# A rank scatter limited by its DMA engines: skipped partitions in five groups, a reset in place of a drain, and ranks from two counts per column

## The chip, the cores and the metric

The kernel runs on one core of a Trainium2 chip. The metric is device time in microseconds (us) per execution. The median before the change is 775.2 us (four runs, 775.0 to 775.73; the first three of them gave 775.31). Smaller is better. Changes are compared with the kernel before on the same chip and in the same rounds. Everything read from a trace comes from one profiled execution of that kernel, and its times count from the start of the span. A run that takes over 1.5% more than the fastest of its kernel is classed slow; ratios use the other runs alone, the fast ones.

## The reference

```python
B, N, D = 8, 2048, 2560                 # x: [B, N, D] fp32, scores: [B, N] fp32

def reference(x, scores):
    order = np.argsort(scores, axis=1)
    ranks = np.argsort(order, axis=1)
    out = np.zeros_like(x)
    b_idx = np.arange(B)[:, None]
    out[b_idx, ranks, :] = x
    return out
```

Each row of 2560 floats (10,240 bytes) goes to the place that its score has in the sorted order of its batch. A row's rank is the number of smaller scores in its batch plus the number of equal scores at smaller positions.

## The kernel before

A batch of 2048 rows is eight groups of 256 rows; a group fills 128 partitions with two rows each. Two kinds of traffic move the rows:

- "Bulk" groups are loaded into one of eight buffers and scattered from there. Pool issues both on one queue, in order, and each scatter waits for the ranks of its batch.
- Group 0 of batches 0 to 5, and the rows of skipped partitions ("holes"), are copied from HBM to HBM one row at a time by the sync engine (SP) and the scalar engine (ACT), 800 rows each. I call them direct rows.

The Vector engine counts the ranks, one column of 128 rows at a time, with every score of the batch spread over all partitions in `s_all`:

```python
THIN = {**{(b, 4): 48 for b in range(1, B)}, (7, 5): 44}   # (batch, group): first skipped partition
HALVED = range(32)                                         # groups loaded in two halves
STEPS = [(0, 1), (1, 2), (2, 4), (4, 8)]                   # groups ranked together, batch 0 only
# ... (cut)
count(0, lo, C, nc.vector.tensor_scalar,                   # later scores: smaller ones
      scalar1=score, scalar2=None, op0=OP.is_lt, op1=OP.add)
if lo:
    count(1, 0, lo, nc.vector.tensor_scalar,               # earlier scores: smaller or equal
          scalar1=score, scalar2=None, op0=OP.is_le, op1=OP.add)
count(2, lo, lo + m, nc.vector.scalar_tensor_tensor,       # equal scores inside the group, masked
      scalar=score, in1=mask[...], op0=OP.is_equal, op1=OP.mult)
# ... (cut)
steps = STEPS if b == 0 else [(0, len(GROUPS))]            # later batches: one step of 16 columns
```

Pool's order of work is one program:

```python
for k in range(1, NBUF):                                   # NBUF = 8 buffers
    load_ahead(k)
for k, (b, g) in enumerate(BULK):
    if k >= LAG and k + NBUF - LAG < len(BULK):            # LAG = 4
        scatters_done(pl, k - LAG)
        load_ahead(k + NBUF - LAG)
    pl.wait(*loaded[k])
    pl.after(dve, t_bulk[b, g])                            # the ranks of (b, g)
    for j in range(GROUPS[g][1]):
        scatter(k, j)
nc.gpsimd.drain()
for k in range(max(0, len(BULK) - NBUF), len(BULK)):
    scatters_done(sp, k)
```

Pool holds everything behind one wait for ranks, loads of later groups too. While it waits, the DMA engines live on what is queued already.

## Time and profile before

| kernel before | |
|---|---|
| time, median | 775.2 us |
| profiled span | 772.8 us |
| rate after the first slice | about 418 GB/s |
| Vector engine busy | 400.7 us, done at about 437 us |
| median landing of the last scatter | 766.6 us, the latest of its sixteen engines 770.6 us |

The page's row of slices divides the span into 40 equal parts; one digit is the busy share in tenths. The prediction shows those rows, the queues, and Pool's wait for batch 1. Beyond them I need the page's line of busy time (engine, us, share of the span, number of instructions) and its costliest group (mean ns of one before the second bar):

```profile
PE 36.2 (5%) x172; PEld 30.4 (4%) x172; DVE 400.7 (52%) x828; ACT 0.0 (0%) x1; POOL 164.6 (21%) x213
L239 DVE TENSOR_SCALAR_CACHE_REDUCE trash<-s_all,s_col 128x1792 bf16<-128x1792 f32 (+7 forms) x240 | 315.2, 1348 | 4.6
```

The counts are most of the Vector engine's work, and no engine is busy for the whole span.

### The profile page before, as it was taken

Reading aid. Unit: us, or ns where it says so; the run is one execution under the profiler, and the core shown is the slowest. Engines: PE = TensorE matmul, PEld = TensorE weight load, DVE = VectorE, ACT = ScalarE, POOL = GpSimd, SP = SyncE. Lnnn points to the kernel's source line nnn. Section 1 sums busy time; section 2 is a strip of 40 time slices with the busy share of each in tenths; the row PEclk is TensorE's granted clock in tenths of the full one; section 3 lists DMA queues with packets and bytes.
Section 4 is the critical chain, followed back from the end, with each engine's and each line's share of the span. In section 5 each row is a group of like instructions: output and inputs, shape, how many; then the busy total and the mean of one; then the engine's idle time right before and its main releaser. Section 6 shows DMA issues by size and latency. Waiting matters only on the chain.

```text
span 772.8 us, 8228 instructions
## 1 busy us (share of the span) xinstructions
PE 36.2 (5%) x172; PEld 30.4 (4%) x172; DVE 400.7 (52%) x828; ACT 0.0 (0%) x1; POOL 164.6 (21%) x213
## 2 busy tenths in 40 slices
PE   4000020020020020030000000000000000000000
PEld 3000010010010010030000000000000000000000
DVE  5999979979979979979999500000000000000000
ACT  0000000000000000000000000000000000000000
POOL 4114223222213131312112121212121212112100
PEclk8555555555555555565555555555555555555555
DMA  8999999999999999999999999999999999999996
GB/s 358 418 418 420 418 418 418 418 417 418 418 420 417 420 417 417 419 417 419 416 421 421 422 416 426 416 427 417 422 417 424 417 426 415 424 418 424 419 414 283
DMA packets 80898, 320.15 MB, mean 414 GB/s; under 512 B 28968, under 2 KB 54568, under 8 KB 54568
## 3 DMA queue, kind: packets, MB, share of 16 engines
q0 software_dynamic: 29376, 300.82, 91.7%
q1 hardware_dynamic: 25904, 10.93, 5.2%
q10 hardware_dynamic: 25600, 8.24, 4.3%
q14 instruction: 17, 0.14, 0.0%
q8 instruction: 1, 0.02, 0.0%
HBM read 168.49 MB, written 168.43 MB: 436 GB/s over the span
## 4 chain that ended last, share of the span: by engine, by line
DMA 63%; DVE 13%; another core or an unknown queue 9%; POOL 6%; issue 4%; PE 1%; POOLq 0%; SPq 0%
DMA out_dram<-x,rank_i 57%; DVE trash L239 12%; DMA x<-in_x_dram 6%; POOL out_dram L424 4%; POOL x L126 2%; PE ps_all L196 0%; DVE s_all L341 0%; DMA s_in<-in_scores_dram 0%; PE ps_col L175 0%; POOLq L448 0%; DVE rank_i L277 0%; DVE rank L271 0%; DVE rank L265 0%; PE ps_row L300 0%
## 5 line engine op out<-in xcount | busy, mean ns | idle before, releaser
L239 DVE TENSOR_SCALAR_CACHE_REDUCE trash<-s_all,s_col 128x1792 bf16<-128x1792 f32 (+7 forms) x240 | 315.2, 1348 | 4.6
L424 POOL DMA_INDIRECT out_dram<-x,rank_i x116 | 113.4, 977 | 139.6 <-issue 35.0
L126 POOL DMA_DIRECT2D x<-in_x_dram x88 | 49.4, 565 | 436.9 <-DMA out_dram<-x,rank_i 418.5
L239 DVE SCALAR_TENSOR_TENSOR trash<-s_all,s_col,mask 128x256 bf16<-128x256 f32 x128 | 61.6, 482 | 0.0
L196 PE MATMUL ps_all<-ident,s_col 128*128 128x128 f32 x128 | 28.1, 411 | 3.2 <-DVE s_all L341 2.8
L300 PE MATMUL ps_row<-ident,rank 128*1 128x128 f32 x28 | 8.3, 398 | 393.6 <-DVE rank_i L286 386.4
L196 PEld LDWEIGHTS ps_all<-ident,s_col 128*128 128x128 f32 x128 | 26.5, 222 | 4.2 <-DVE s_all L341 3.2
L341 DVE COPY s_all<-ps_all 128x512 f32<-128x512 f32 x32 | 20.2, 685 | 1.5 <-PE ps_all L196 1.1
L239 DVE DVE_READ_ACCUMULATOR trash<-s_all,s_col 128x1 f32 x240 | 19.9, 83 | 0.0
L300 PEld LDWEIGHTS ps_row<-ident,rank 128*1 128x1 f32 x28 | 2.0, 97 | 397.9 <-DVE rank_i L286 389.5
L311 DVE TENSOR_SCALAR thin_i<-ps_row 1x8 int32<-1x8 f32 x8 | 1.2, 154 | 19.0 <-PE ps_row L300 19.0
L239 DVE DVE_READ_ACCUMULATOR trash<-s_all,s_col,mask 128x1 f32 x128 | 10.7, 83 | 0.0
L326 DVE TENSOR_SCALAR rows_i<-ps_row 1x256 int32<-1x256 f32 x6 | 2.5, 412 | 4.1 <-PE ps_row L300 4.1
L183 DVE COPY s_col<-ps_col 128x128 f32<-128x128 f32 x1 | 0.3, 293 | 4.7 <-PE ps_col L175 4.7
L175 PE MATMUL ps_col<-ident,s_in 8*128 8x8 f32 x16 | 2.1, 262 | 3.9 <-DMA s_in<-in_scores_dram 3.9
L286 DVE TENSOR_SCALAR rank_i<-rank,hole 128x2 int32<-128x2 f32 x8 | 2.1, 262 | 0.3
L175 PEld LDWEIGHTS ps_col<-ident,s_in 8*128 8x128 f32 x16 | 2.0, 211 | 3.9 <-DMA s_in<-in_scores_dram 3.9
L277 DVE CAST rank_i<-rank 128x16 int32<-128x16 f32 (+3 forms) x11 | 1.9, 173 | 0.4
L271 DVE TENSOR_TENSOR rank<-rank,acc 128x16 f32<-128x16 f32 (+3 forms) x11 | 1.9, 171 | 0.4
L265 DVE TENSOR_TENSOR rank<-acc,acc 128x16 f32<-128x16 f32 (+3 forms) x11 | 1.9, 170 | 0.4
L156 POOL TENSOR_SCALAR_AFFINE_SELECT mask<-mask 128x256 f32<-128x256 f32 x2 | 0.8, 398 | 0.0
L168 DVE MEMSET acc<- 128x128 f32 x1 | 0.2, 165 | 1.1 <-SPq L102 1.1
(10 smaller groups left out, 1.8 us busy)
## 6 DMA issues: line engine op xcount, KB each, us to landing
x<-in_x_dram POOLq DMA_DIRECT2D x62, 1280.0 KB
x<-in_x_dram POOLq DMA_DIRECT2D x26, 2560.0 KB
out_dram<-in_x_dram ACTq DMA_DIRECT2D x800, 10.0 KB
out_dram<-in_x_dram SPq DMA_DIRECT2D x800, 10.0 KB
x<-in_x_dram SPq DMA_DIRECT2D x2, 1280.0 KB, 9.1
out_dram<-x,rank_i POOLq DMA_INDIRECT x116, 49.0
s_in<-in_scores_dram SPq DMA_DIRECT2D x1, 64.0 KB
```

The costliest lines, as they stand in the source:

```text
L126: line.eng.dma_start(out=xb[k % NBUF][:, part], in_=rows[:, part]).then_inc(sem, 16)
L175: nc.tensor.transpose(out=ps_col[:, B * c:B * (c + 1)], in_=s_in[:, r + j:r + m * P:m], identity=ident[:B, :B],)
L196: nc.tensor.transpose(out=ps_all[:, P * c:P * (c + 1)], in_=s_col[:, c, b:b + 1].to_broadcast([P, P]), identity=ident[:],)
L239: do(out=trash[i][:, :P * (hi_c - lo_c)], in0=s_all[:, P * lo_c:P * hi_c], accum_out=acc[i][:, col:col + 1], **how,)
L265: nc.vector.tensor_tensor(out=rank[:, cols], in0=acc[0][:, cols], in1=acc[1][:, cols], op=OP.add)
L271: nc.vector.tensor_tensor(out=rank[:, cols], in0=rank[:, cols], in1=acc[2][:, cols], op=OP.add)
L277: nc.vector.tensor_copy(out=rank_i[:, cols], in_=rank[:, cols])
L286: nc.vector.tensor_scalar(out=rank_i[:, cols], in0=rank[:, cols], scalar1=hole[:, i:i + 1], scalar2=None, op0=OP.add,)
L300: nc.tensor.transpose(out=ps_row[:1, P * j:P * (j + 1)], in_=rank[:, col:col + 1], identity=ident[:],)
L326: nc.vector.tensor_scalar(out=rows_i[b][:].rearrange("o (p j) -> o p j", p=P), in0=ps_row[:1, :WIDE].rearrange("o (j p) -> o p j", p=P), s ...
L341: nc.vector.tensor_copy(out=s_all[:, 512 * q:512 * (q + 1)], in_=ps_all[:, 512 * q:512 * (q + 1)],)
L424: nc.gpsimd.indirect_dma_start(out=out_flat, out_offset=bass.IndirectOffsetOnAxis(ap=rank_i[:, col:col + 1], axis=0), in_=xb[k % NBUF][:, ...
```

## The change

It has three parts with separate intents. The skipped partitions are meant to even out the DMA engines: fewer groups have a hole, but now the load skips it too, by a gathered load whose indices run out of bounds at the hole. The reset at the end is meant to cost less than the drain. Two counts in place of three are meant to spare Vector instructions: one count of all smaller scores, and one masked count of equal scores from the batch's start up to the column.

```diff
-    THIN = {**{(b, 4): 48 for b in range(1, B)}, (7, 5): 44}
+    THIN = {**{(b, 4): 48 for b in range(1, B, 2)}, (7, 5): 44}
+    THIN_LOADS = [k for k in THIN if k[0]]
-    HALVED = range(32)
+    HALVED = range(34)
 ...
-    mask = pool.tile([P, 2 * MMAX, P], F32, name="mask")
+    mask = pool.tile([P, C + 2 * MMAX, P], BF16, name="mask")
 ...
         def load(line, k, sem):
+            if (b, g) in THIN_LOADS:
+                i = HOLES.index(THIN[b, g])
+                line.after(dve, t_thin[0])
+                nc.gpsimd.indirect_dma_start(
+                    out=xb[k % NBUF][:, :m * D], out_offset=None,
+                    in_=x.rearrange("b (q j) d -> (b q) (j d)", j=m),
+                    in_offset=bass.IndirectOffsetOnAxis(ap=thin_row[:, i:i + 1], axis=0),
+                    element_offset=(b * N + r) * D,
+                    bounds_check=P - 1, oob_is_err=False,
+                ).then_inc(sem, 16)
+                ...
+                return
 ...
                     count(
-                        0, lo, C, nc.vector.tensor_scalar,
+                        0, 0, C, nc.vector.tensor_scalar,
                         scalar1=score, scalar2=None, op0=OP.is_lt, op1=OP.add,
                     )
-                    if lo:
-                        count(
-                            1, 0, lo, nc.vector.tensor_scalar,
-                            scalar1=score, scalar2=None, op0=OP.is_le, op1=OP.add,
-                        )
+                    first = C + MMAX - j - lo
                     count(
-                        2, lo, lo + m, nc.vector.scalar_tensor_tensor,
+                        1, 0, lo + m, nc.vector.scalar_tensor_tensor,
                         scalar=score,
-                        in1=mask[:, MMAX - j:MMAX - j + m, :].rearrange("p a b -> p (a b)"),
+                        in1=mask[:, first:first + lo + m, :].rearrange("p a b -> p (a b)"),
                         op0=OP.is_equal, op1=OP.mult,
                     )
 ...
-        nc.gpsimd.drain()
-
         for k in range(max(0, len(BULK) - NBUF), len(BULK)):
-            scatters_done(sp, k)
+            scatters_done(pl, k)
+
+        nc.gpsimd.dma_reset()
```

Cut: the two Vector instructions that make `thin_row`, one addition of partial ranks that falls away, the memsets of the wider mask, and a rewritten loop of the direct rows whose new branch is unused (`FLAT = ()`).

## The prediction

> **What bounds the kernel now.** I read the page's totals, slices and queues first, to see whether an engine or the transfers fill the span; then busy time by stretch; then Pool's order of time around the one long wait I found, beside the Vector engine's order there; last the groups by form, for prices.
>
> ```profile
> span 772.8 us, 8228 instructions
> DVE  5999979979979979979999500000000000000000
> DMA  8999999999999999999999999999999999999996
> GB/s 358 418 418 420 418 418 418 418 417 418 418 420 417 420 417 417 419 417 419 416 421 421 422 416 426 416 427 417 422 417 424 417 426 415 424 418 424 419 414 283
> q0 software_dynamic: 29376, 300.82, 91.7%
> q1 hardware_dynamic: 25904, 10.93, 5.2%
> q10 hardware_dynamic: 25600, 8.24, 4.3%
> ```
>
> The three queues together fill 101% of sixteen DMA engines, and 418 GB/s stands from 19 us to the last slice. The transfers are the bound; the Vector engine works until about 437 us and is hidden, but only while the DMA queue has work.
>
> ```profile
> 75.00:127.00 52.00, 4.43 (x20) 3.75 (x20) 47.19 (x97) 0.00 (x0) 13.44 (x18) 0.53 1.03 418
> 760.00:767.00 7.00, 0.00 (x0) 0.00 (x0) 0.00 (x0) 0.00 (x0) 0.00 (x0) 0.50 0.90 376
> 767.00:772.80 5.80, 0.00 (x0) 0.00 (x0) 0.00 (x0) 0.00 (x0) 0.00 (x0) 0.50 0.06 25
> ```
>
> These are stretches; the last two columns are DMA share and GB/s. Full at 75 to 127 us; a thin tail of slow engines after 767.
>
> ```profile
> 84.46 1.13 POOL L126 DMA_DIRECT2D x<-in_x_dram  x2 [2.93 <-DMA out_dram<-x,rank_i]
> 111.26 0.99 POOL L424 DMA_INDIRECT out_dram<-x,rank_i  x1 [25.66 <-DVE rank_i L286]
> ```
>
> ```profile
> 110.28 0.17 DVE L277 CAST rank_i<-rank 128x16 int32<-128x16 f32 x1
> ```
>
> Pool queues nothing between 85.6 and 111.3 us: it waits for the ranks of batch 1. This is the one place where the Vector engine may set the pace. Groups by form (mean ns last before the bar):
>
> ```profile
> L239 DVE TENSOR_SCALAR_CACHE_REDUCE trash<-s_all,s_col 128x2048 bf16<-128x2048 f32 x16 | 37.5, 2346 | 0.6
> L239 DVE TENSOR_SCALAR_CACHE_REDUCE trash<-s_all,s_col 128x256 bf16<-128x256 f32 x32 | 15.3, 477 | 0.6
> L239 DVE SCALAR_TENSOR_TENSOR trash<-s_all,s_col,mask 128x256 bf16<-128x256 f32 x128 | 61.6, 482 | 0.0
> ```
>
> **What the Trainium skill says.** "VectorE: DVE Perf Modes", section on the perf-mode tier table: a two-tensor operation on fp32 runs at one element a cycle. The trace agrees: the masked count, 482 ns for 256, costs what the scalar count costs, 477. The same table gives tensor_scalar on fp32 twice that rate, 1227 ns for 2048; here the counting form takes 2346, so I use the measurement. "DMA: Bandwidth & Descriptors", "The descriptor swizzle": partitions 44 to 47 belong to engine 3 and 48 to 51 to engine 4. The trace has no engine numbers, but of the sixteen landings of each scatter two come late, up to 6 us behind the median, and these drop back by about 3 us at the groups with a hole: it fits. "HBM Reference", "Access": a lone core reaches about 425 GB/s, bounded by its DMA engines; measured 418.
>
> **The change, part by part.**
>
> *Holes.* Groups that skip four partitions fall from eight to five, and their loads skip them too. A packet of 10,240 bytes takes 385 ns in the trace, one of 20,480 takes 761. Engine 4: before, 7 groups x 8 scatter rows = 56 packets saved; after, 4 groups x (8 scatter rows + 4 double load rows) = 64 equivalents: 8 x 0.385 = 3.1 us less. Engine 3: 8 packets saved before, 16 after: 3.1 us less. The rows copied directly fall from 64 to 40; each costs every engine a 640-byte packet (32 ns) and a 4-byte one (9 ns): 24 x 0.041 = 1.0 us less on all. Two more groups loaded in halves, and the gathered loads in whole packets, cancel within 0.2 us.
> The last scatter before lands at a median of 766.6 us; one engine at 768.1, and two at 769.4 and 770.6 (times after the span's start, from the trace's landings). I take those two for engines 4 and 3. By this part alone the last landing would be max(766.6-1.0, 768.1-1.0, 769.4-4.1, 770.6-4.1) = 767.1: a gain of 3.5 us.
>
> *Reset in place of the drain.* The last landing is at 770.6, the drain ends at 771.9 and the span 0.9 later. The reset comes after Pool's own waits for the landings; I guess 0.2 us for it instead of 1.35: gain 1.1 us.
>
> *Ranks.* A column takes a full count and a masked count. Start to start in the trace: 2.28 us for 2048 elements, 0.52 for the masked 256. Slope of the scalar count (2346-477)/1792 = 1.043 ns an element, so 0.267 us for every further 256. Before, two scalar counts and one mask: 2.93 us a column in all but the first two (2.80). After, column pair g takes 2.80 + 0.267 g each. A batch of sixteen columns: 16 x 2.80 + 2 x 28 x 0.267 = 59.8 us, against 2 x 2.80 + 14 x 2.93 = 46.6: plus 13.2 us a batch, although instructions are fewer. One small addition per step (0.2 us) goes.
> Batch 0, in steps, from 10.66: first pair to 16.26, rows to 17.7, step two 6.13 us, step three 13.87, step four 34.15, with 0.4 us between steps: ranks at 73.1 (before 60.7). Then 0.5 us for the row indices of the gathered loads, 2.5 us of copies, 59.8 us of counts: the cast of batch 1 ends at about 136.3 and Pool's scatter follows 0.8 us later as before, at 137.0 instead of 111.3.
>
> *How long does the queue last?* Before that scatter Pool has queued 12 loads and 7 scatter groups of 2.62 MB, and about 224 direct rows have moved: 49.8 + 2.3 = 52.1 MB. The first slice moves 6.9 MB; the rest at 418 GB/s takes 108.1 us: empty at 127.4. The landings of the twelfth load agree: about 128.2 for the typical engine, 129.6 and 132 for the late two. So before the change there are 17 us in hand, and the change takes 25.7. With 1 us of issue and a first byte about 1 us later ("DMA: Bandwidth & Descriptors", Specifications, for transfers from GpSimd; the trace shows it only for Pool's first load, 3.9 us after issue but beside other loads, so I allow half a microsecond more), data flow again at 139.5. A typical engine loses 139.5 - 128.2 = 11.3 us; direct rows use about 0.5 of it. The late engines, being behind, lose less: about 9.9 (engine 3) and 7.5 (engine 4), and all start again level. The wait at 73.1 costs 1 to 2 us of idleness that lies inside this same count, since the later gap is measured from the old time of emptying.
> Later batches: ranks come every 62 to 65 us, a group takes 13.1 us and a batch of seven 92. Batch 2 at about 204 is issued some 13 us late, but in steady state a scatter waits over 40 us in the queue (median issue to landing 49.0), so nothing runs dry.
>
> *Sum.* Typical engine: 766.6 + 11.3 - 0.5 - 1.0 = 776.4. The slightly late one: 768.1 + 11.1 - 0.5 - 1.0 = 777.7. Engine 3: 770.6 + 9.9 - 0.5 - 4.1 = 775.9. Engine 4: 769.4 + 7.5 - 0.5 - 1.0 = 775.4 (its saving in the gathered load of batch 1 falls before the gap and is lost; after it, 21.6 us are saved in both kernels). Last landing 777.7, plus 0.2 and 0.9: span 778.8, that is 6 us more; time 775.3 + 6.0 = 781.3, which I round down to 781.0.
>
> **Rivals.** (1) The Vector engine stays hidden and only the balance counts: gains of 3.5 and 1.1, time about 770.7. For it: the DMA row is 9 everywhere and the queue 40 us deep later. Against it: the 25.7 us wait at batch 1, with only 17 in hand. It would need masked counts at double rate. (2) The gap costs more: a restart of 4 us after issue, or gathered rows cut into smaller packets; five gathered loads at half rate would add some 5 x 6 = 30 us to one stretch each, partly seen as time: 786 to 800. For it: nothing in this trace gathers. Against: the scatter moves whole 10 KB rows by the same kind of issue. (3) The end is set by something that paces all engines together, the slowest engine holding back Pool through its waits. Then relief of engines 3 and 4 pays in full and the gap, which realigns them, costs about 8: 774 to 777. For it: a lag that stays at 6 us after 440 us. Against: the DMA share is 1.01 to 1.03 there, no idleness. (4) The reset walks through many semaphores and is no cheaper than the drain: plus 1.
>
> **Range and chances.** Gap 8 to 13, balance gain between 1 and 4, tail gain 0 to 1.2: 775 to 786 should hold it eight times in ten. Two per cent is 15.5 us; only rival 2 reaches it upwards, and nothing downwards, since the bytes fall by only 0.3%.
>
> **What would show it.** Right: Pool's scatter of batch 1 issued near 137 after a wait near 50 us; a slice between 127 and 140 us with the DMA share well under 1 and lower GB/s; Vector busy near 500 us, ending near 530; masked counts of 2048 near 2.35 us; no drain tail after the last landing; the last sixteen landings within about 2 us instead of 4.6. Wrong: no dip in GB/s there, masked counts much faster, or gathered loads with many small packets.

## More of the kernel before

The view by stretch: the columns are the stretch, its length, the busy time of PE, PEld, DVE, ACT and POOL with instruction counts, the granted clock, the DMA share and GB/s.

```profile
75.00:93.00 18.00, 0.00 (x0) 0.00 (x0) 17.79 (x37) 0.00 (x0) 4.23 (x6) 0.50 1.02 417
127.00:140.00 13.00, 0.00 (x0) 0.00 (x0) 12.86 (x27) 0.00 (x0) 2.67 (x4) 0.50 1.03 418
140.00:158.00 18.00, 0.00 (x0) 0.00 (x0) 17.79 (x37) 0.00 (x0) 5.74 (x8) 0.50 1.02 418
```

Full rate in all three. The changed kernel is read in the same stretches below.

## The result, and the profile after

The changed kernel takes 782.43 us (median of four runs, 782.28 to 782.73) against 775.2. A ratio here is the mean time of one kernel's fast runs over that of the other's of the same rounds, so it is not quite the ratio of the medians: 1.0093, interval 1.0075 to 1.011. It is slower by 7.2 us, within two per cent. The page after, with the lines that answer to those shown of before:

```profile
span 780.9 us, 7925 instructions
PE 34.4 (4%) x166; PEld 29.6 (4%) x166; DVE 504.5 (65%) x589; ACT 0.0 (0%) x1; POOL 176.4 (23%) x213
DVE  6999999799999799999989999991000000000000
DMA  8999997999999999999999999999999999999998
GB/s 360 418 419 402 396 419 271 348 420 421 417 418 419 417 416 422 418 417 418 417 420 418 421 426 413 424 415 425 416 426 416 423 417 424 416 424 416 426 412 349
L262 DVE TENSOR_SCALAR_CACHE_REDUCE trash<-s_all,s_col 128x2048 bf16<-128x2048 f32 x128 | 300.3, 2346 | 4.6
L262 DVE SCALAR_TENSOR_TENSOR trash<-s_all,s_col,mask 128x512 bf16<-128x512 f32 (+7 forms) x128 | 181.1, 1415 | 0.0
```

The Vector engine runs 239 instructions fewer (589 against 828) and is busy 104 us longer. Every column now pays 2346 ns for the full count, and the masked counts average 1415 ns where they were 482. The digit of the DMA row falls below 9 in the seventh slice (117 to 137 us), and GB/s falls in four slices: 402 and 396 between 59 and 98 us, and 271 and 348 between 117 and 156 us. Around that time Pool's lines are these (start, length, engine, line, operation; in brackets the idle time before it and who ended it):

```profile
73.69 0.95 POOL L466 DMA_INDIRECT out_dram<-x,rank_i  x1 [29.35 <-DVE thin_row L359]
...
83.65 1.04 POOL L135 DMA_INDIRECT x<-in_x_dram,thin_row  x1 [0.30 <-issue]
...
87.23 1.15 POOL L149 DMA_DIRECT2D x<-in_x_dram  x2
136.81 1.00 POOL L466 DMA_INDIRECT out_dram<-x,rank_i  x1 [48.43 <-DVE rank_i L299]
```

Pool waits 48.4 us for the ranks of batch 1, where it waited 25.7, and queues nothing between 88.4 and 136.8 us. The Vector engine's own order of time shows that it was computing until then:

```profile
133.23 2.35 DVE L262 SCALAR_TENSOR_TENSOR trash<-s_all,s_col,mask 128x2048 bf16<-128x2048 f32 x1
...
135.83 0.17 DVE L290 CAST rank_i<-rank 128x16 int32<-128x16 f32 x1
```

Its last masked count covers 2048 elements and costs 2.35 us, as much as a full count. The stretches:

```profile
75.00:93.00 18.00, 0.00 (x0) 0.00 (x0) 17.78 (x23) 0.00 (x0) 11.24 (x14) 0.50 1.02 380
93.00:127.00 34.00, 0.00 (x0) 0.00 (x0) 33.68 (x37) 0.00 (x0) 0.00 (x0) 0.50 1.02 420
127.00:140.00 13.00, 3.67 (x18) 3.59 (x19) 9.54 (x12) 0.00 (x0) 2.89 (x4) 0.50 0.43 148
140.00:158.00 18.00, 0.75 (x4) 0.16 (x2) 17.00 (x24) 0.00 (x0) 11.82 (x15) 0.59 1.02 380
776.00:780.90 4.90, 0.00 (x0) 0.00 (x0) 0.00 (x0) 0.00 (x0) 0.00 (x0) 0.50 0.30 127
```

From 93 to 127 us the queue's stock keeps the DMA engines full although Pool issues nothing. From 127 to 140 us it is spent: share 0.43, 148 GB/s. In the trace's packet records the bulk queue moves nothing between 129.6 and 138.4 us. The two stretches at 380 GB/s are another matter: their share is 1.02. The share counts time in which packets are under way, so it does not fall when packets are slow. The records show it: a packet of 10,240 bytes takes 386 ns on average elsewhere, but 415 to 438 ns in the successive 6 us pieces from 74 to 92 us, and 498, 397 and 400 ns from 140 to 158 us. Both stretches follow directly after Pool's queue ran empty or nearly so: when Pool went on at 73.7 us, the last scatter queued before landed 1.6 us later.

What the three stretches lose against 418 GB/s can be added up: (418 − 148) × 13 / 418 = 8.4 us, and (418 − 380) × 18 / 418 = 1.6 us twice. That is 11.7 us. The landings agree: the first scatter of batch 1 lands 10 to 11 us later than before, the third group 12.1 us later, and the last scatter's typical engine (the median of its sixteen landings) at 777.6 instead of 766.6 us, 11.0 us later.

At the end, the four latest engines land at 778.6, 779.0, 779.5 and 779.6 us; before, at 767.6, 768.0, 769.3 and 770.6. The latest is 2.0 us behind the typical engine, where it was 4.0 behind. The reset follows the last landing at once and takes 0.30 us; before, the drain ended 1.35 us after the last landing. From the last landing to the end of the span it is 1.3 us, where it was 2.2.

### The profile page after: what moved, and what is told of

It is laid out like the page before. It is cut to its first block, busy times and chain, and to the rows that moved or that the text cites. A ratio compares the mean times of both kernels' runs of the same rounds, so it can differ in the third digit from the quotient of the medians.

```text
span 780.9 us, 7925 instructions
## 1 busy us (share of the span) xinstructions
PE 34.4 (4%) x166; PEld 29.6 (4%) x166; DVE 504.5 (65%) x589; ACT 0.0 (0%) x1; POOL 176.4 (23%) x213
## 4 chain that ended last, share of the span: by engine, by line
DMA 66%; DVE 16%; another core or an unknown queue 6%; POOL 5%; issue 3%; PE 1%; POOLq 0%; SPq 0%
DMA out_dram<-x,rank_i 60%; DVE trash L262 15%; DMA x<-in_x_dram 6%; POOL out_dram L466 3%; POOL x L149 1%; POOL x L135 1%; PE ps_all L219 0%; DVE s_all L374 0%; DMA s_in<-in_scores_dram 0%; PE ps_col L198 0%; DVE rank_i L290 0%; DVE rank L284 0%; PE ps_row L313 0%; DVE rows_i L339 0%
## 5 line engine op out<-in xcount | busy, mean ns | idle before, releaser
L262 DVE TENSOR_SCALAR_CACHE_REDUCE trash<-s_all,s_col 128x2048 bf16<-128x2048 f32 x128 | 300.3, 2346 | 4.6
L262 DVE SCALAR_TENSOR_TENSOR trash<-s_all,s_col,mask 128x512 bf16<-128x512 f32 (+7 forms) x128 | 181.1, 1415 | 0.0
L466 POOL DMA_INDIRECT out_dram<-x,rank_i x116 | 122.8, 1059 | 185.7 <-DVE rank_i L299 48.4
L149 POOL DMA_DIRECT2D x<-in_x_dram x83 | 46.7, 565 | 349.4 <-DMA out_dram<-x,rank_i 328.7
L313 PE MATMUL ps_row<-ident,rank 128*1 128x128 f32 x22 | 6.3, 389 | 490.7 <-DVE rank_i L299 357.9
L135 POOL DMA_INDIRECT x<-in_x_dram,thin_row x5 | 5.2, 1031 | 38.4 <-DMA out_dram<-x,rank_i 38.1
L262 DVE DVE_READ_ACCUMULATOR trash<-s_all,s_col 128x1 f32 x128 | 10.6, 83 | 0.0
L324 DVE TENSOR_SCALAR thin_i<-ps_row 1x8 int32<-1x8 f32 x5 | 0.8, 153 | 10.9 <-PE ps_row L313 10.9
L191 DVE MEMSET mask<- 128x2048 bf16 x1 | 1.8, 1765 | 1.5 <-SPq L109 1.5
## 6 DMA issues: line engine op xcount, KB each, us to landing
out_dram<-x,rank_i POOLq DMA_INDIRECT x116, 47.9
x<-in_x_dram,thin_row POOLq DMA_INDIRECT x5, 33.6
```

The costliest lines, as they stand in the source:

```text
L135: nc.gpsimd.indirect_dma_start(out=xb[k % NBUF][:, :m * D], out_offset=None, in_=x.rearrange("b (q j) d -> (b q) (j d)", j=m), in_offset=b ...
L149: line.eng.dma_start(out=xb[k % NBUF][:, part], in_=rows[:, part]).then_inc(sem, 16)
L191: dve.did(nc.vector.memset(mask[:, :C, :], 1.0))
L262: do(out=trash[i][:, :P * (hi_c - lo_c)], in0=s_all[:, P * lo_c:P * hi_c], accum_out=acc[i][:, col:col + 1], **how,)
L313: nc.tensor.transpose(out=ps_row[:1, P * j:P * (j + 1)], in_=rank[:, col:col + 1], identity=ident[:],)
L466: nc.gpsimd.indirect_dma_start(out=out_flat, out_offset=bass.IndirectOffsetOnAxis(ap=rank_i[:, col:col + 1], axis=0), in_=xb[k % NBUF][:, ...
```

## The experiments

The theory (A): the holes and the reset gain about 4 us. The longer ranks cost about 11 us, all of it in one place, because the wait for batch 1 outlasts the queued transfers; the Vector engine's work after that is hidden. Rivals: (B) the gathered loads are slow; (C) more Vector work costs time everywhere, or two counts disturb the transfers in some other way; (D) the end is paced by the slowest engine, so that the parts do not add up. Twelve kernels ran; all gave the reference's result. The expectations have letters of their own: C is there that the balance was misjudged, and R that the direct rows end last.

### First group, on one chip: the parts alone (before: 775.8 us)

**e1_three_counts**, the changed kernel with the old counts:

```diff
 # against the changed kernel
-    count(0, 0, C, ... is_lt)
-    count(1, 0, lo + m, ... is_equal x mask)
+    count(0, lo, C, ... is_lt)
+    if lo:
+        count(1, 0, lo, ... is_le)
+    count(2, lo, lo + m, ... is_equal x mask)
```

> The changed kernel with the three counts per column put back (holes and reset kept). Theory A, the queue of transfers runs dry once because the ranks of batch 1 come late: no gap, so the gains of the other two parts stand alone, 771 us (3.5 + 1.1 us under the kernel before), scatter of batch 1 again near 111 us. Theory B, the gathered loads or the holes cost the time: 780 us or more stays. Theory C, the balance was misjudged and only the tail gains: 774.

Measured: 772.31 us (771.3 to 772.38), ratio 0.9949 (0.9936 to 0.9962). Its rate by slice:

```profile
span 770.3 us, 8160 instructions
GB/s 358 418 417 419 417 420 418 417 418 419 417 417 419 418 417 421 418 418 417 419 419 417 426 415 425 416 424 416 424 416 424 417 424 417 422 420 419 424 413 320
```

No slice dips, and Pool's wait for batch 1 is 26.0 us again. The holes and the reset together gain 3.9 us by the ratio, so in the changed kernel the two counts cost 7.2 + 3.9, about 11.1 us. No steady kernel has a lower median (e4, below, is within its interval); it beats both.

**e2_two_counts_only**, the kernel before with nothing but the new counts:

```diff
 # against the kernel before
-    count(0, lo, C, ... is_lt)
-    if lo:
-        count(1, 0, lo, ... is_le)
-    count(2, lo, lo + m, ... is_equal x mask)
+    count(0, 0, C, ... is_lt)
+    count(1, 0, lo + m, ... is_equal x mask)
```

> The kernel before with the two counts alone (old holes, old drain). Theory A: gap at 129 to 139 us with the DMA share near 0.2, the late engines keep their lag of before less what the gap gives back, 784 to 785 us. Theory B: no more than 776. Theory C (nothing gained by the holes): 783 or less, that is the changed kernel plus 1.1.

Measured: 787.41 us (786.47 to 789.54), ratio 1.0157 (1.0144 to 1.017), plus 12.2 us. This is 2 to 3 us more than I expected. The same gap is in its stretches:

```profile
75.00:93.00 18.00, 0.00 (x0) 0.00 (x0) 17.78 (x25) 0.00 (x0) 11.41 (x15) 0.50 1.01 371
127.00:140.00 13.00, 3.99 (x20) 3.59 (x20) 9.22 (x12) 0.00 (x0) 3.11 (x4) 0.52 0.50 180
140.00:158.00 18.00, 0.00 (x1) 0.00 (x0) 17.71 (x26) 0.00 (x0) 11.49 (x14) 0.58 1.02 382
```

Nothing gathers here, so rival B is not needed for the gap or for the slow stretches. Its last scatter landed at 779.9 us, but the last direct row at 783.3 us: the rows, not the bulk, ended last, which may be the 2 to 3 us. That was new. In the kernel before the rows have landed at 764 us, some 6 us ahead of the bulk; in the changed kernel at 775, still ahead of 779.6.

**e3_steps_b1**, the changed kernel with batch 1 ranked in four steps, so that its first scatter need not wait for all 16 columns:

```diff
-            steps = STEPS if b == 0 else [(0, len(GROUPS))]
+            steps = STEPS if b <= 1 else [(0, len(GROUPS))]
```

> The changed kernel, but batch 1 also gives out its ranks in four steps as batch 0 does, so that its first scatters can be issued near 88 us instead of 137. Theory A: the Vector engine does the same work plus about 1 us, yet the gap disappears and the time is 770 to 772. A rival in which the longer counts slow the transfers all along (two streams read from memory at once): still 778 or more.

Measured: 776.83 us median of seven runs, widely spread (775.24 to 789.19); ratio of the fast runs 1.0013 (0.9997 to 1.003). A miss: I expected 770 to 772. The profiled run, at 789.19, was slow, so its length explains nothing by itself; I use it only to see what ended last. The rate by slice, and what was still under way at the end:

```profile
GB/s 359 420 417 402 390 419 413 419 418 419 416 419 421 415 420 419 419 418 419 417 418 420 418 424 417 422 419 421 424 405 420 421 420 422 418 423 417 419 411 26
```

```profile
754.54 29.88 SPq L439 DMA_DIRECT2D out_dram<-in_x_dram  x34
755.08 22.62 ACTq L439 DMA_DIRECT2D out_dram<-in_x_dram  x27
```

The gap is gone: slices seven and eight stand at 413 and 419. The bulk's last landing is at 770.0 us, as theory A has it. But direct rows went on until 786 us, in a last slice at 26 GB/s. SP issues 34 rows in 29.9 us there, 0.88 us each, with the DMA engines nearly idle. So the rows are a chain of their own. In the traces the median step from one row to the next on a queue is 0.74 us in most kernels, and every 16 rows their addresses are read for 1 to 4 us more. The mean step is 0.89 to 0.98 us, so that the 784 to 800 rows of a queue (six direct groups) take 713 to 774 us.

**e4_holes_only**, the kernel before with the new holes and the gathered loads alone:

```diff
 # against the kernel before
-    THIN = {**{(b, 4): 48 for b in range(1, B)}, (7, 5): 44}
+    THIN = {**{(b, 4): 48 for b in range(1, B, 2)}, (7, 5): 44}
+    THIN_LOADS = [k for k in THIN if k[0]]
-    HALVED = range(32)
+    HALVED = range(34)
 # and the gathered load, as in the change
```

> The kernel before with the five gathered groups alone. If engines 3 and 4 are the two late ones and the typical engine gains 1.0 us: 3.5 us less, 771.7. If the slow engines pace all through Pool's waits: 4 us less or more. If the gather costs: more than 775.

Measured: 772.7 us (772.21 to 774.61), ratio 0.9958 (0.9945 to 0.9971), minus 3.3 us. As expected. The profiled run was the slowest of the five, and in it direct rows landed last, at 771.6 us. Its scatters show where a gain is: the typical engine lands at 766.4 us, only 0.2 earlier than before, and the four latest at 766.6, 766.7, 768.1 and 768.3. The two latest engines gained 1.2 and 2.2 us. Gathered loads are not slow: in the changed kernel they land 33.6 us after issue at the median, plain loads after 42 to 45 and scatters after 47.9, the time in the queue included. Rival B falls.

### Second group, on one chip: time taken from the ranks, without any other change (before: 775.26 us)

**e5_delay_small** and **e6_delay_large** put useless full counts ahead of batch 1's ranks, into a spare tile, in the kernel before: four and eleven. In the traces they move Pool's scatter of batch 1 by 9.4 and by 26.5 us.

```diff
 # against the kernel before; 4 in the one, 11 in the other
+            for _ in range(4 if b == 1 else 0):
+                dve.after(dve, dve.n)
+                dve.did(nc.vector.tensor_scalar(
+                    out=trash[0][:], in0=s_all[:], accum_out=idle[:],
+                    scalar1=s_col[:, 0, b:b + 1], scalar2=None, op0=OP.is_lt, op1=OP.add))
```

> The kernel before with four useless counts of 2048 elements ahead of the ranks of batch 1: 9.6 us more on the Vector engine there, so Pool's first scatter of batch 1 near 121 us, some 7 us before the queue would be empty. Theory A, the queue runs dry only beyond 17 us of delay: no change, within 1 us of before. A rival in which every microsecond of delay of batch 1 counts: plus 9.

> The same with eleven useless counts, 26 us, as much delay of batch 1 as the change brings, with the counts of before and without its late scatters at 73 us. Theory A: a gap at 129 to 139 us and 9 to 11 us more than before, 785. Rival, the longer two-stream counts or the gathered loads themselves cost the time: no change.

Measured: the small delay 776.11 us (775.26 to 777.3), ratio 1.0008 (0.9995 to 1.0021), no change, although Pool's scatter of batch 1 moved from 111.3 to 120.6 us. The large one 786.68 us (785.78 to 787.57), ratio 1.014 (1.0125 to 1.0156), plus 10.9 us, with the scatter at 137.7 us. First two lines of the small delay, the scatter and the stretch that follows it:

```profile
120.64 0.99 POOL L433 DMA_INDIRECT out_dram<-x,rank_i  x1 [35.64 <-DVE rank_i L287]
120.00:134.00 14.00, 4.42 (x20) 3.75 (x20) 9.75 (x16) 0.00 (x0) 11.23 (x14) 0.50 1.02 418
```

Then the scatter and the stretches of the large one:

```profile
137.73 0.99 POOL L433 DMA_INDIRECT out_dram<-x,rank_i  x1 [52.61 <-DVE rank_i L287]
75.00:93.00 18.00, 0.00 (x0) 0.00 (x0) 17.71 (x19) 0.00 (x0) 4.24 (x6) 0.50 1.02 416
127.00:140.00 13.00, 2.75 (x14) 2.67 (x15) 10.36 (x27) 0.00 (x0) 1.97 (x2) 0.50 0.24 71
140.00:158.00 18.00, 1.40 (x8) 1.04 (x6) 16.35 (x28) 0.00 (x0) 12.50 (x17) 0.59 1.02 381
```

This is the threshold that theory A needs and rival C cannot have: 9.4 us of lateness at this place are free, 26.5 us cost 10.9. The cause is lateness alone, since the counts, masks and holes are the old ones. In the profiled run of the large delay direct rows landed last, at 783.7 us, so its time is not the bulk's alone; but the bulk shows the cost too: its last scatter landed at 780.6 us, 10.0 later than before, and its typical engine at 778.6, 12.1 later. The slow restart (381 GB/s at a share of 1.02) comes with it, so it too belongs to the emptied queue. At 75 to 93 us, where this kernel's queue was not empty, the rate is full. In the small delay Pool issued as fast from 120.6 us on, with the queue's stock good for some 8 us more, and the rate stayed at 418 GB/s: a burst of issues alone does not slow the packets.

**e7_two_counts_late**, the changed kernel with three counts in batches 0 and 1 and two from batch 2 on:

```diff
 # against the changed kernel
+                    if b < 2:
+                        count(0, lo, C, ... is_lt)
+                        if lo:
+                            count(1, 0, lo, ... is_le)
+                        count(2, lo, lo + m, ... is_equal x mask)
+                        continue
```

> The changed kernel with three counts in batches 0 and 1 and two counts from batch 2 on: 79 of the 105 us of added Vector work stay. Theory A: it is hidden, 772 us like the run with three counts everywhere, and no slice under 410 GB/s before the last. Rival, the added counts cost wherever they stand: 779 or more.

Measured: two of eight runs fast (771.26 and 776.72 us), six slow (784 to 819). Ratio of the fast ones 0.9978 (0.9946 to 1.001). The expected steady 772 did not come. In the profiled run, again a slow one, the last stretches are:

```profile
755.00:765.00 10.00, 0.00 (x0) 0.00 (x0) 0.00 (x0) 0.00 (x0) 0.00 (x0) 0.50 0.90 360
765.00:780.00 15.00, 0.00 (x0) 0.00 (x0) 0.00 (x0) 0.00 (x0) 0.00 (x0) 0.50 0.14 25
780.00:796.90 16.90, 0.00 (x0) 0.00 (x0) 0.00 (x0) 0.00 (x0) 0.00 (x0) 0.50 0.06 12
```

The bulk is done at 765.1 us, the earliest of all kernels. The rest is direct rows at 12 to 25 GB/s. Whether the two counts are hidden in late batches is therefore left to e9.

**e8_reset_only**, the kernel before with the reset:

```diff
 # against the kernel before
-        nc.gpsimd.drain()
-
         for k in range(max(0, len(BULK) - NBUF), len(BULK)):
-            scatters_done(sp, k)
+            scatters_done(pl, k)
+
+        nc.gpsimd.dma_reset()
```

> The kernel before with Pool's waits and the reset in place of the drain alone: the tail after the last landing shrinks from 2.2 to 1.3 us, so 0.7 to 1.1 us faster, 774.9. If the reset is no cheaper: no change.

Measured: 775.12 us (774.12 to 777.66), ratio 0.9988 (0.9975 to 1.0), minus 0.9 us. The interval reaches 1, so the gain is barely resolved. The reset itself took 0.30 us in the trace. In this profiled run (the slowest of the five) direct rows landed until 774.2 us, 3 us after the bulk, so the shorter tail of the changed kernel (1.3 us for 2.2) shows the gain better.

### Third group, on one chip: the same questions with the rows out of the way (before: 775.85 us)

e3 and e7 could not answer because direct rows set their end. Three kernels therefore copy group 0 directly in five batches, not six; the sixth goes through the bulk queue.

```diff
-    DIRECT = range(6)
+    DIRECT = range(5)
```

**e9_late_relief** is e7 with this edit, **e10_steps_relief** is e3 with it, **e11_after_relief** the changed kernel with it.

> The run with two counts from batch 2 on, whose time spread from 771 to 819 us, with five directly copied groups instead of six. Theory R: there the end is set by the direct rows, which two sequencers issue one by one at 0.95 to 1 us each (792 rows from 19 us on), not by the bulk, which ended at 765. With 128 rows fewer on each queue the rows end near 670 us; the bulk grows by one group, 12.3 us per engine against 10.5 for its rows, so 1.8 us: 771 to 774, and all runs within 2 us of each other. Rival: the added counts disturb the transfers themselves: the spread and times over 780 stay.

> The changed kernel with batch 1 in four steps, and five direct groups. Theories A and R together: no gap and no row tail, bulk at 770 plus 1.8, so 773 to 776, steady. If the stepwise ranks had another cost: 780 or spread.

> The changed kernel with five direct groups alone: the control for the two others. The gap at 129 to 138 us stays and the bulk sets the end: 782.4 plus 1.8, 784; 9 us above the stepwise one. If the rows were what set the end of the changed kernel: 780 or less.

Measured:

| kernel | median | range | ratio to before |
|---|---|---|---|
| e9_late_relief | 776.93 us | 775.55 to 777.54 | 1.0002 (0.9975 to 1.0028) |
| e10_steps_relief | 778.44 us | 777.54 to 779.94 | 1.0027 (1.0 to 1.0054) |
| e11_after_relief | 789.38 us | 788.34 to 789.76 | 1.0163 (1.0136 to 1.0189) |

All runs are fast and steady now, which the row theory asked for: e7's kernel was slow in six of eight runs, e9 in none of six. The levels lie some 2 to 5 us above what I expected, in all three, because the relief costs more than the 1.8 us that I had put down (the changed kernel was 7.2 us over before, e11 is 13.5 over). The differences between them need no such term. e10 and e11 differ only in the steps of batch 1:

```profile
75.00:93.00 18.00, 4.00 (x18) 3.52 (x18) 16.98 (x27) 0.00 (x0) 13.27 (x16) 0.91 1.02 379
127.00:140.00 13.00, 0.59 (x2) 0.09 (x2) 12.11 (x15) 0.00 (x0) 0.45 (x1) 0.50 1.02 419
140.00:158.00 18.00, 0.00 (x0) 0.00 (x0) 17.79 (x25) 0.00 (x0) 7.87 (x10) 0.50 1.02 418
```

```profile
75.00:93.00 18.00, 0.00 (x0) 0.00 (x0) 17.79 (x23) 0.00 (x0) 11.00 (x14) 0.50 1.02 386
127.00:140.00 13.00, 3.70 (x20) 3.30 (x20) 9.44 (x14) 0.00 (x0) 3.12 (x4) 0.54 0.44 148
140.00:158.00 18.00, 0.00 (x0) 0.00 (x0) 17.78 (x25) 0.00 (x0) 11.59 (x14) 0.56 1.02 378
```

The first fence is e10, the second e11. Splitting one wait in four fills the gap and removes the second slow stretch; the first, at 75 to 93 us, stays in both. The times differ by 10.9 us. That is what the wait for batch 1 costs in the changed kernel, measured with the end free of rows, and by the stretches it is (418 − 148) × 13 / 418 + (418 − 378) × 18 / 418 = 8.4 + 1.7 = 10.1 us. e9, with two counts in six of eight batches, lies 12.5 us below e11, so those counts are hidden to within what these runs resolve. It also lies 1.5 us below e10, which fits the slow stretch at 75 to 93 us that e10 keeps (1.7 us). Rival C falls.

**e12_hole_moved**, the kernel before with the last hole at partition 60, to see whether the latest engine is the one that the hole at 44 relieves:

```diff
 # against the kernel before
-    THIN = {**{(b, 4): 48 for b in range(1, B)}, (7, 5): 44}
+    THIN = {**{(b, 4): 48 for b in range(1, B)}, (7, 5): 60}
```

> The kernel before with the single hole of batch 7 moved from partitions 44 to 47 to partitions 60 to 63: engine 3 loses 3.1 us of relief[...]. If engine 3 is the last one before, as the prediction took it: the last landing 3.1 us later, 778.4. If engine 3 is not the late one: 775.5.

Measured: 777.14 us (776.32 to 781.48), ratio 1.0017 (0.9986 to 1.0048). The value lies between the two expectations and the interval holds 1: inconclusive. The last landing was 772.0 us instead of 770.6, half of the shift that I had worked out. Which engine is the latest stays open.

## Why the prediction was right

It said 781.0 us; the measured time is 782.43. The mechanism held, and some of its terms were off in both directions.

- **The prices of the counts: right.** The full count and the masked count of 2048 take 2.35 us, and the engine is busy 504.5 us where I had said near 500.
- **The moment of the wait: right.** Pool's scatter of batch 1 came at 136.81 us (predicted 137.0), after 48.4 us.
- **The stock in hand: right.** The prediction had the queue empty at 127.4 to 128.2 us and 17 us in hand. It ran empty at 129.6 us; e5 shows that 9.4 us are within the stock, e6 that 26.5 us are not.
- **The restart: mis-sized.** I had data again at 139.5 us, and 11.3 us lost by a typical engine. Bulk data flowed at 138.4 us, 1.6 us after Pool began to issue; I had allowed 2.5. The pause was 8.8 us.
- **The slow stretches: missing from the sum.** The queue restarts at 380 GB/s for some 18 us, twice: 1.6 us each. I had said that the wait at 73.1 us lies inside the later count; its idleness may, but its slow packets do not: e10 keeps them with the later gap gone. The omission and the smaller pause nearly cancel, which is luck: 8.4 + 3.3 = 11.7 us, where the sum had 11.3 less 0.5 for the direct rows, 10.8.
- **The holes: right in the sum, not resolved in the parts.** Minus 3.3 us in e4 (predicted 3.5). The typical engine was to gain 1.0 us and landed 0.2 earlier, but single traces do not resolve this: in e8, with the rows and holes of before, it landed 0.4 earlier. e11 suggests that a direct row costs less than the 41 ns put down. A group of 256 rows through the bulk is 5.24 MB, an estimated 12.5 us at 418 GB/s; the relief cost about 6.3 us net by the times (13.5 − 7.2), 4.8 by the typical engine's landing (782.5 against 777.6), so its rows had cost about 6 to 8 us, an estimated 24 to 30 ns each. The latest engine landed 2.2 us earlier in e4. That the end is level now, within about 2 us, was predicted and came. Which engine is which was not shown (e12).
- **The reset: about right.** 0.30 us where 0.2 was guessed; gain 0.9 against 1.1, barely resolved in e8's times and seen in the tail (2.2 to 1.3 us).
- **The sum.** The typical engine was to land last at 776.4 us and did so at 777.6. By the landings of batch 1's third group the gap with its slow stretches cost 12.1 us where the sum had 11.3, and from there to the end 1.1 us was won back where 1.5 was predicted. The latest was to land 1.3 us behind it and came 2.0 behind, at 779.6 (predicted 777.7). With 1.3 us to the end of the span that makes 780.9 (predicted 778.8). The profiled spans differ by 8.1 us, the medians by 7.2, since the profiled run before was faster than its kernel's timed runs (774.87) and the one after the slowest of its kernel's (782.73); so the error in the time is 1.4 us.
- **Rival 1** (all hidden, 770.7) fell with e6; e1 shows what that time would have been. **Rival 2** (slow gathers) fell with e4, except that a slow restart exists: nine per cent below the full rate, and without gathers too (e2, e6). **Rival 3** (slowest engine paces all, 774 to 777), which is D above, fell with the typical engine's 11.0 us. **Rival 4** (a dear reset) fell with the 0.30 us.
- **Not foreseen: a second chain.** The prediction treated direct rows as load on the DMA engines. Issued one at a time they are also a chain that ends within 7 us of the bulk. It was not the end of the changed kernel, so the prediction did not suffer. In the profiled runs of e2, e3, e4, e6, e7 and e8, though, the rows landed last, and in e3 and e7 they hid the gain.

Two readings of the prediction are slightly off. The 425 GB/s stand in the section "Specifications (TRN2)" of "HBM Reference", just above "Access". And the drop of a late engine at a group with a hole, put at about 3 us, is 1.8 to 2.9 us in the trace before.

Two things stay open. Why packets are slow after the queue has run empty: Pool then issues just ahead of the transfers, which would fit, but no run separates this from a queue that is empty as such; e5 only excludes the burst of issues by itself. And why the pace of the direct rows differs between kernels and runs.

## What to carry to other kernels

Count the stock: where one engine issues all transfers and waits for another's result, work out how long the queued bytes last, and compare that with the wait before and after the change; below the stock extra work was free here, above it about each microsecond was paid. Fewer instructions are no saving when each covers more elements, so price the elements, and if a wait must grow, split it so that the first consumer can start. Read GB/s beside the DMA share, because slow packets keep the share full, and look for a second chain that ends a few microseconds before the first.

## What the Trainium skill lacked or had wrong

- "VectorE: DVE Perf Modes", the perf-mode tier table: it gives tensor_scalar on fp32 1227 ns for 2048 elements. In its counting form, with a sum taken along, it took 2346 ns in every one of 128 instructions here. The table has no row for this form; that the form of tensor_scalar which also writes out its accumulator is not among those that can enter the faster two-port modes is said elsewhere, in "SBUF — State Buffer", Who interferes with whom. Nor has it a row for the masked count (scalar_tensor_tensor, fp32 with a bf16 mask), which took 2.35 us for 2048.
- "DMA: Bandwidth & Descriptors", Specifications: a first byte after about 1 us for transfers from GpSimd. This agrees roughly: 1.6 us from the start of Pool's issue, 0.6 after its end, on an idle queue. That the packets after such a restart are slow is on no page that I read: 397 to 498 ns in place of 386 for 10,240 bytes, 380 GB/s in place of 418 for about 18 us, at an unchanged DMA share of 1.02.
- "DMA: Bandwidth & Descriptors", Issuing engines are not separate DMA queues: it calls the time to initiate a DMA usually small beside the DMA. For single rows of 10,240 bytes it was the larger: 0.74 us a row on one queue at the median, with the address reads 0.89 to 0.98 us on average, while an estimated 24 to 41 ns of all sixteen DMA engines carry a row. In the profiled runs of six experiments this chain ended last.
- No page that I read prices the reset: 0.30 us after the last landing, against 1.35 us from the last landing to the end of a drain.
